# Combining two expert outputs: two input tiles' results in one 32 KB store row, an early table load, last stores from SyncE

## The chip, the cores and the metric

The kernel runs on one core of a Trainium2 chip. The core has several engines, each with its own instruction stream: TensorE (not used here), VectorE (DVE in the profile), ScalarE (ACT), GpSimd (POOL) and SyncE (SP). Data moves between the chip's main memory (HBM) and the on-chip memory SBUF, which has 128 partitions, by 16 transfer engines (DMA). SyncE and ScalarE each have a queue of their own for such transfers; the instructions that issue them are marked SPq and ACTq in the profile.

The metric is the time of one execution in device microseconds, as a median over runs. Before the change it is 241.34 us (three runs, 241.24 to 241.75). The profiled execution, from its first to its last instruction, spans 240.1 us.

## The reference

```python
batch, seq, hidden, n_experts, k = 16, 1024, 512, 8, 2
"expert_outputs": np.random.randn(batch, seq, k, hidden).astype(np.float32)
"combine_weights": np.random.randn(batch, seq, k).astype(np.float32)

def reference(expert_outputs, combine_weights):
    weights = combine_weights[..., np.newaxis]
    return np.sum(expert_outputs * weights, axis=2).astype(np.float32)
```

Each of the 16 x 1024 = 16384 tokens has two vectors of 512 floats. The output is the first times a weight plus the second times another weight. 67.1 MB are read and 33.6 MB written for two multiplications and one addition per output element.

## The kernel before

The 16384 tokens are dealt out to the partitions: partition p holds the tokens p x 128 to p x 128 + 127 (`per` = 128). One token's two vectors are 4 KB next to each other in memory, and one partition's tokens follow each other.

The outer loop (line 45) runs over 16 tiles `g` of `J` = 8 tokens per partition. A tile's input `et` is 128 partitions x 32 KB, 4096 KB in all; it is loaded by one transfer that SyncE issues (line 48). In main memory one partition's part of it is a single run of 32 KB, and the transfer goes as 128 such rows, 8 on each of the 16 transfer engines. A tile's output `ot` is 128 partitions x 16 KB and leaves in one transfer of 128 rows of 16 KB, issued by ScalarE (line 66). The pools (lines 39 and 40) hold four input tiles and four output tiles, 128 + 64 KB of each partition.

For each token of a tile VectorE multiplies the first vector by its weight into `ot` (line 57, TENSOR_SCALAR), and then adds the second vector times its weight (line 58, SCALAR_TENSOR_TENSOR). The weights are in `wt`, 1 KB per partition, which ScalarE's queue loads at the start (line 43). In the last tile the multiplication is ScalarE's (line 55, ACTIVATE with the weight as scale), so that two engines share that tile; and that tile leaves in three stores of 4, 2 and 2 tokens, as soon as each part is done. ScalarE's first activation needs a table, whose load (ACT_TABLE_LOAD) stands right before it in the instruction stream.

A framework puts in the waits. An engine works through its own instructions in the order of the program text, apart from small exchanges among independent ones on VectorE. SyncE issues the first four loads at once; the load of tile g + 4 waits until VectorE has done with tile g. ScalarE issues the store of a tile when VectorE has written all of it; whatever stands behind it on ScalarE waits with it. In each queue the transfers start in the order of issue.

Of the kernel before, what the change touches and what calls it, by code (L numbers as in the profile page):

```python
# [1 line left out]

# [4 lines left out]


@with_exitstack
def kernel(  # L10
    ctx: ExitStack,
    tc: tile.TileContext,
    expert_outputs: bass.AP,
    combine_weights: bass.AP,
    out: bass.AP,
):


    nc = tc.nc
    b, s, k, h = expert_outputs.shape  # L20
    assert k == 2
    n = b * s
    P = nc.NUM_PARTITIONS
    per = n // P
    assert per * P == n
    eo = expert_outputs.rearrange("b s k h -> (b s) (k h)").rearrange("(p t) f -> p t f", p=P)
    cw = combine_weights.rearrange("b s k -> (b s) k").rearrange("(p t) k -> p (t k)", p=P)
    o = out.rearrange("b s h -> (b s) h").rearrange("(p t) f -> p t f", p=P)

    dt = mybir.dt.float32  # L30
    mult = mybir.AluOpType.mult
    add = mybir.AluOpType.add

    J = 8
    copy = mybir.ActivationFunctionType.Copy
    last = per // J - 1

    wpool = ctx.enter_context(tc.tile_pool(name="w", bufs=1))
    ipool = ctx.enter_context(tc.tile_pool(name="in", bufs=4))
    opool = ctx.enter_context(tc.tile_pool(name="out", bufs=4))  # L40

    wt = wpool.tile([P, per * k], dt)
    nc.scalar.dma_start(out=wt, in_=cw)

    for g in range(per // J):
        et = ipool.tile([P, J, k * h], dt)
        ot = opool.tile([P, J, h], dt)
        nc.sync.dma_start(out=et, in_=eo[:, g * J : (g + 1) * J, :])  # L48
        c0 = 0
        for c in (4, 2, 2) if g == last else (J,):  # L50
            for i in range(c0, c0 + c):
                t = g * J + i
                w0, w1 = wt[:, 2 * t : 2 * t + 1], wt[:, 2 * t + 1 : 2 * t + 2]
                if g == last:
                    nc.scalar.activation(out=ot[:, i, :], in_=et[:, i, 0:h], func=copy, scale=w0)  # L55
                else:
                    nc.vector.tensor_scalar_mul(out=ot[:, i, :], in0=et[:, i, 0:h], scalar1=w0)  # L57
                nc.vector.scalar_tensor_tensor(  # L58
                    out=ot[:, i, :],
                    in0=et[:, i, h : 2 * h],  # L60
                    scalar=w1,
                    in1=ot[:, i, :],
                    op0=mult,
                    op1=add,
                )
            nc.scalar.dma_start(  # L66
                out=o[:, g * J + c0 : g * J + c0 + c, :], in_=ot[:, c0 : c0 + c, :]
            )
            c0 += c


# [1 line left out]
_INS = ['expert_outputs', 'combine_weights']  # L73
_OUTS = [((16, 1024, 512), 'float32')]


# [23 lines left out]
```

## Time and profile before

| | |
|---|---|
| time, median of three runs | 241.34 us |
| span of the profiled execution | 240.1 us |
| VectorE busy | 133.8 us (56%) |
| ScalarE busy | 6.4 us (3%) |
| bytes moved | 100.81 MB, 420 GB/s over the span |
| VectorE, line 57 | 120 times, 482 ns each |
| VectorE, line 58 | 128 times, 746 ns each |
| ScalarE, line 55 | 8 times, 709 ns each, and a table load of 1283 ns |
| first compute | at 13.92 us |
| last load's data used from | 227.81 us |

The profile page has six parts: busy times by engine; the span in 40 slices of 6 us each, with the transfer engines' busy share in tenths and the GB/s that they moved; the transfer queues; the chain of work that ended last; the costliest groups of instructions, with the idle time before them and what ended it; and the transfer issues, with the time from issue to landing. An engine that idles much may still not matter: what counts is what the chain at the end waits for. A stretch of the span can be asked for by itself; its row gives busy times, transfer share and GB/s in that stretch. Transfers are counted there at the start of each row, so that a stretch of few microseconds can show a share a little above 1.

### The profile page before, as it was taken

The numbers are of one execution on the slowest core, as the hardware profiler recorded it, in microseconds if no ns is written. First come the engines' busy times: TensorE is split into PE (matmuls) and PEld (weight loads), VectorE is DVE, ScalarE is ACT, GpSimd is POOL, SyncE is SP. The second block draws the span as 40 slices with busy tenths as digits, with TensorE's granted clock in tenths as the row PEclk, the third lists the DMA queues.
The fourth block names the chain that finished last, engine by engine and source line by source line (L and its number), as shares of the span: only waits on it lengthen the run. The fifth ranks groups of instructions, "written<-read, shape, count | busy, mean of one in ns | idle before, by whom it ended". The sixth has DMA issues, their size and how long they took to land.

```text
span 240.1 us, 377 instructions
## 1 busy us (share of the span) xinstructions
DVE 133.8 (56%) x248; ACT 6.4 (3%) x9; POOL 0.2 (0%) x4
## 2 busy tenths in 40 slices
DVE  0068937729185490945819276391853919549062
ACT  0000000000000000000000000000000000000072
POOL 0000000000000000000000000000000000000000
DMA  7999999999999999999999999999999999999967
GB/s 267 439 434 431 355 434 456 414 431 437 437 423 445 439 409 426 456 415 453 420 437 431 415 448 423 431 450 437 435 423 434 420 429 442 418 450 437 412 296 304
DMA packets 5042, 100.81 MB, mean 420 GB/s; under 512 B 560, under 2 KB 688, under 8 KB 944
## 3 DMA queue, kind: packets, MB, share of 16 engines
q1 hardware_dynamic: 2304, 67.11, 65.4%
q10 hardware_dynamic: 2736, 33.69, 32.9%
q14 instruction: 2, 0.02, 0.0%
HBM read 67.24 MB, written 33.55 MB: 420 GB/s over the span
## 4 chain that ended last, share of the span: by engine, by line
DMA 56%; DVE 26%; another core or an unknown queue 13%; issue 1%; ACT 1%; SPq 0%; ACTq 0%; DVEq 0%
DMA et<-in_expert_outputs_dram 56%; DVE ot L58 16%; DVE ot L57 10%; ACT ot L55 1%; ACT L55 1%; SPq L48 0%; ACTq L66 0%; DVEq L95 0%; DVEq L57 0%; ACTq L55 0%
## 5 line engine op out<-in xcount | busy, mean ns | idle before, releaser
L57 DVE TENSOR_SCALAR ot<-et,wt 128x512 f32<-128x512 f32 x120 | 52.7, 482 | 93.4 <-DMA et<-in_expert_outputs_dram 79.5
L58 DVE SCALAR_TENSOR_TENSOR ot<-et,wt,ot 128x512 f32<-128x512 f32 x128 | 90.0, 746 | 9.3 <-ACT ot L55 9.3
L55 ACT ACT_TABLE_LOAD x1 | 1.3, 1283 | 227.8 <-DMA et<-in_expert_outputs_dram 227.8
L55 ACT ACTIVATE ot<-et,wt 128x512 f32<-128x512 f32 x8 | 5.1, 709 | 1.5 <-DVE ot L58 1.5
L84 POOL MEMSET const-bfloat16-1.0<- 128x1 bf16 x1 | 0.1, 101 | 0.0
L84 POOL MEMSET const-uint8-127<- 128x1 uint8 x1 | 0.1, 101 | 0.0
L84 POOL MEMSET const-float32-0.0<- 128x1 f32 x1 | 0.1, 98 | 0.2 <-issue 0.2
L84 POOL MEMSET const-float32-1.0<- 128x1 f32 x1 | 0.1, 98 | 0.0
## 6 DMA issues: line engine op xcount, KB each, us to landing
et<-in_expert_outputs_dram SPq DMA_DIRECT2D x16, 4096.0 KB, 49.6
out_dram<-ot ACTq DMA_DIRECT2D x15, 2048.0 KB, 24.9
out_dram<-ot ACTq DMA_DIRECT2D x1, 1024.0 KB, 3.9
out_dram<-ot ACTq DMA_DIRECT2D x2, 512.0 KB, 3.2
wt<-in_combine_weights_dram ACTq DMA_DIRECT2D x1, 128.0 KB, 13.2
```

The lines of the kernel that those rows point to most:

```text
L55: nc.scalar.activation(out=ot[:, i, :], in_=et[:, i, 0:h], func=copy, scale=w0)
L57: nc.vector.tensor_scalar_mul(out=ot[:, i, :], in0=et[:, i, 0:h], scalar1=w0)
L58: nc.vector.scalar_tensor_tensor(out=ot[:, i, :], in0=et[:, i, h : 2 * h], scalar=w1, in1=ot[:, i, :], op0=mult, op1=add,)
L84: nc = _bacc.Bacc("TRN2", target_bir_lowering=False, num_devices=1)
```

## The change

The change has four parts.

- **Two tiles in one store.** An output tile now holds the results of two input tiles (128 partitions x 32 KB). ScalarE stores it in one transfer of rows of 32 KB when the second of the two tiles is done. There are seven such stores, for tiles 0 to 13. Tile 14 leaves alone, with rows of 16 KB, and tile 15 in four stores of 2 tokens each (rows of 4 KB). The purpose is fewer and longer rows.
- **Three input and three double output tiles** in place of four and four, 96 + 96 KB of each partition, so that the same room suffices.
- **Table loaded early.** The first token of tile 0 is multiplied on ScalarE, so that the table load stands near the start and no longer ahead of the last tile.
- **Last stores from SyncE.** The four stores of tile 15 are issued by SyncE, which has no loads left by then. ScalarE doesn't wait for VectorE between its multiplications of the last tile.

```diff
+    STORES = {t: 2 * J for t in range(2 * J, per, 2 * J)}
+    STORES[per - J] = J
+    STORES.update({t: 2 for t in range(per - J + 2, per + 1, 2)})
...
-    ipool = ctx.enter_context(tc.tile_pool(name="in", bufs=4))
-    opool = ctx.enter_context(tc.tile_pool(name="out", bufs=4))
+    ipool = ctx.enter_context(tc.tile_pool(name="in", bufs=3))
+    opool = ctx.enter_context(tc.tile_pool(name="out", bufs=3))
...
     for g in range(per // J):
         et = ipool.tile([P, J, k * h], dt)
-        ot = opool.tile([P, J, h], dt)
         nc.sync.dma_start(out=et, in_=eo[:, g * J : (g + 1) * J, :])
-        c0 = 0
-        for c in (4, 2, 2) if g == last else (J,):
-            for i in range(c0, c0 + c):
...
-                if g == last:
...
+        if g % 2 == 0:
+            ot = opool.tile([P, 2 * J, h], dt)
+        at = g % 2 * J
+        for i in range(J):
+            t = g * J + i
...
+            if t == 0 or g == last:
+                nc.scalar.activation(out=ot[:, at + i, :], in_=et[:, i, 0:h], func=copy, scale=w0)
+            else:
+                nc.vector.tensor_scalar_mul(out=ot[:, at + i, :], in0=et[:, i, 0:h], scalar1=w0)
...
+            c = STORES.get(t + 1)
+            if c:
+                (nc.sync if g == last else nc.scalar).dma_start(
+                    out=o[:, t + 1 - c : t + 1, :], in_=ot[:, at + i + 1 - c : at + i + 1, :]
                 )
-            nc.scalar.dma_start(
-                out=o[:, g * J + c0 : g * J + c0 + c, :], in_=ot[:, c0 : c0 + c, :]
-            )
-            c0 += c
```

More of the change, by code (lines that the diff above doesn't have):

```diff
@@ L32 @@
     add = mybir.AluOpType.add
+    copy = mybir.ActivationFunctionType.Copy
     J = 8
-    copy = mybir.ActivationFunctionType.Copy
     last = per // J - 1
+    STORES = {t: 2 * J for t in range(2 * J, per, 2 * J)}
+    STORES[per - J] = J
+    STORES.update({t: 2 for t in range(per - J + 2, per + 1, 2)})
     wpool = ctx.enter_context(tc.tile_pool(name="w", bufs=1))
-    ipool = ctx.enter_context(tc.tile_pool(name="in", bufs=4))
-    opool = ctx.enter_context(tc.tile_pool(name="out", bufs=4))
+    ipool = ctx.enter_context(tc.tile_pool(name="in", bufs=3))
+    opool = ctx.enter_context(tc.tile_pool(name="out", bufs=3))
     wt = wpool.tile([P, per * k], dt)
@@ L46 @@
         et = ipool.tile([P, J, k * h], dt)
-        ot = opool.tile([P, J, h], dt)
         nc.sync.dma_start(out=et, in_=eo[:, g * J : (g + 1) * J, :])
-        c0 = 0
-        for c in (4, 2, 2) if g == last else (J,):
-            for i in range(c0, c0 + c):
-                t = g * J + i
-                w0, w1 = wt[:, 2 * t : 2 * t + 1], wt[:, 2 * t + 1 : 2 * t + 2]
-                if g == last:
[L55 to L64, printed above, removed]
-                )
-            nc.scalar.dma_start(
-                out=o[:, g * J + c0 : g * J + c0 + c, :], in_=ot[:, c0 : c0 + c, :]
-            )
-            c0 += c
+        if g % 2 == 0:
[3 more added lines that the diff above has]
+            t = g * J + i
+            w0, w1 = wt[:, 2 * t : 2 * t + 1], wt[:, 2 * t + 1 : 2 * t + 2]
+            if t == 0 or g == last:
+                nc.scalar.activation(out=ot[:, at + i, :], in_=et[:, i, 0:h], func=copy, scale=w0)
+            else:
+                nc.vector.tensor_scalar_mul(out=ot[:, at + i, :], in0=et[:, i, 0:h], scalar1=w0)
+            nc.vector.scalar_tensor_tensor(
+                out=ot[:, at + i, :],
+                in0=et[:, i, h : 2 * h],
+                scalar=w1,
+                in1=ot[:, at + i, :],
+                op0=mult,
+                op1=add,
+            )
+            c = STORES.get(t + 1)
+            if c:
+                (nc.sync if g == last else nc.scalar).dma_start(
+                    out=o[:, t + 1 - c : t + 1, :], in_=ot[:, at + i + 1 - c : at + i + 1, :]
+                )
 _INS = ['expert_outputs', 'combine_weights']
```

## The prediction, before the result was known

> **What bounds the kernel now.** First I read the page's busy times, slices and queues, to see whether an engine or the transfers fill the span. In the queue lines the last column is time in the transfer engines, as a share of 16 engines' span; q1 holds the loads (SyncE), q10 the table and the stores (ScalarE).
>
> ```profile
> DVE 133.8 (56%) x248; ACT 6.4 (3%) x9; POOL 0.2 (0%) x4
> ...
> DMA  7999999999999999999999999999999999999967
> GB/s 267 439 434 431 355 434 456 414 431 437 437 423 445 439 409 426 456 415 453 420 437 431 415 448 423 431 450 437 435 423 434 420 429 442 418 450 437 412 296 304
> ...
> q1 hardware_dynamic: 2304, 67.11, 65.4%
> q10 hardware_dynamic: 2736, 33.69, 32.9%
> ```
>
> VectorE is busy 56%; the transfer engines are busy 65.4 + 32.9 = 98.3%. Only the first slice, the fifth (355) and the last two fall short. So I read those by stretches (columns: stretch, its length, busy us of the engines with their instruction counts, TensorE clock, transfer engines' busy share, GB/s).
>
> ```profile
> 6.00:23.00 17.00, 8.56 (x16) 0.00 (x0) 0.00 (x0) 1.00 1.01 436
> 23.00:28.00 5.00, 4.54 (x9) 0.00 (x0) 0.00 (x0) 1.00 0.94 344
> 28.00:227.80 199.80, 115.27 (x216) 0.00 (x0) 0.00 (x0) 1.00 1.00 432
> 227.80:231.40 3.60, 1.55 (x3) 3.58 (x5) 0.00 (x0) 1.00 1.01 432
> 231.40:233.40 2.00, 2.00 (x4) 1.48 (x3) 0.00 (x0) 1.00 0.14 57
> 233.40:240.10 6.70, 1.94 (x3) 1.33 (x2) 0.00 (x0) 1.00 0.77 313
> ```
>
> From 28 to 227.8 us, when the last load lands, the rate is flat at 432 GB/s with the share at 1.00. Two places stand out: 23 to 28 us, where the engines count as busy but move only 344, and the hole at 231.4 to 233.4. The tail itself is in the order of time (start, duration, engine, line):
>
> ```profile
> 221.78 0.34 ACTq L66 DMA_DIRECT2D out_dram<-ot  x1
> 227.81 1.28 ACT L55 ACT_TABLE_LOAD   x1 [227.81 <-DMA et<-in_expert_outputs_dram]
> 229.10 3.78 ACT L55 ACTIVATE ot<-et,wt 128x512 f32<-128x512 f32 x6
> 229.85 4.07 DVE L58 SCALAR_TENSOR_TENSOR ot<-et,wt,ot 128x512 f32<-128x512 f32 x6 [8.11 <-ACT ot L55]
> 232.63 1.66 ACTq L66 DMA_DIRECT2D out_dram<-ot  x2
> 234.34 1.33 ACT L55 ACTIVATE ot<-et,wt 128x512 f32<-128x512 f32 x2 [1.46 <-DVE ot L58]
> ```
>
> The table load stands on the path, and ScalarE waits in its own store issues before the last two multiplies. Finally the issues with their time to landing:
>
> ```profile
> et<-in_expert_outputs_dram SPq DMA_DIRECT2D x16, 4096.0 KB, 49.6
> out_dram<-ot ACTq DMA_DIRECT2D x15, 2048.0 KB, 24.9
> ```
>
> **Prices.** One transfer engine carries 8 rows of each transfer (128 partitions over 16 engines). A 32 KB load row: 65.4% of 240.1 us is 157.0 us, by 128 rows = 1.227 us. A 16 KB store row: 32.9% is 79.0, less about 5.4 for the table and the small last stores, by 120 = 0.613 us. The packet records of the trace have medians of 1.213, 0.611, 0.313 (8 KB) and 0.160 us (4 KB), which I use. One input tile with one store is 8 x (1.213 + 0.611) = 14.6 us, which is the spacing of the tiles in the chain (37.76, 52.36). A store lands 24.9 us after issue, longer than 14.6: so **the next store is always queued before the last has drained**; ScalarE's queue never runs empty between 23 us and the tail.
>
> **What the Trainium skill says.** DMA: Bandwidth & Descriptors, "Queues, rings and completion order", has each transfer engine taking turns between the queue rows that have work, a packet at a time. The trace agrees: 8 load rows with 8 store rows make the 14.6 us. It follows that the row size sets the shares: 2:1 for the loads now, 1:1 with 32 KB store rows. The same page, "Where 436 GB/s comes from", gives a ceiling of 435 GB/s; measured are 432 to 436, so nothing is left in the steady part. "Issuing engines are not separate DMA queues" there says that another issuing engine saves only issue time (here 0.33 to 0.36 us). ScalarE: Activation LUTs, "What ACT_TABLE_LOAD costs", gives about 1283 ns and a drain of about 1380; the trace has 1283 ns and no gap after it (229.10 follows 227.81 + 1.28). No page says what it costs a busy transfer engine when a queue goes from empty to filled.
>
> **The change, part by part.**
>
> *Double stores.* Per transfer engine 112 rows of 16 KB become 56 of 32 KB. Two 16 KB rows cost 2 x 0.611 = 1.222, one of 32 KB 1.213: 56 x 0.009 = **0.5 us less**, on the path, since the engines are the bound. In the last tile 4 stores of 4 KB rows (32 x 0.160 = 5.12) replace 8 x 0.313 + 16 x 0.160 = 5.06: 0.06 us more.
>
> *The double stores' rhythm.* A pair of tiles is 16 load rows and 8 store rows, 24 x 1.213 = 29.1 us. A store, one for one with loads, is through in 16 x 1.213 = 19.4 us, and then the queue is **empty for 9.7 us** until the next. So it fills from empty seven times, where before it did once (22.51 us). What that once cost is visible: 23 to 28 us moved 344 instead of 432 GB/s, 5 x (1 - 344/432) = 1.0 us lost. Packet records: at that place the load rows on all 16 engines stretch from 1.21 to as much as 2.0 us, 0.72 us of extra time per engine, and this ahead of the first store row, so before store data moves. The instruction queue's two 8 KB fetches (47.4 and 173.7 us) each likewise stretch the load row behind them, by 0.54 and 0.60 us. Against it: the store queue starts only once beside loads in this trace, so it may be a first-time cost. Bounds: 0 to 1.0 us a restart; I take 0.72. Six more restarts: **+4.3 us** (0 to 6).
>
> *Three input tiles.* A load now waits for VectorE three tiles back. VectorE takes 8.5 us a tile (13.92 to 22.45), and loads alone bring a tile in 8 x 1.213 = 9.7 us. While tile g is computed, g+1 and g+2 are queued, 19.4 us of work for loads alone: the load queue doesn't empty. Cost nothing, hidden by the queued loads. The third double output tile back has landed tens of us before VectorE writes it again. Semaphores shared among transfers add waits on SyncE for older stores; by the order of the instructions each is for one issued at least 30 us earlier. Nothing.
>
> *Table early.* 1.28 us leaves 227.81 and lies beside the first tile, where VectorE starts with rows 1 and 2 and needs ScalarE's row later. *Last stores from SyncE.* ScalarE's 8 multiplies then run through (0.63 us apart) and VectorE ends about 8 x 0.67 + 0.75 = 6.1 us after the last load; before it was 236.5 - 227.8 = 8.7. That takes 2.6 us off the compute path. But how much of it counts? At the last load's landing some 4.2 MB remain (store of tile 14 and all of tile 15), 9.7 us at 432: the transfers, not ScalarE, end last. What is saved is their hole. And the hole (0.14 busy for 2 us) is not one on all engines: the records show one engine, the one delayed by the instruction fetches, busy through to 233.36, and idle then for only 0.1 us and 0.25 us at 237.3. The slowest engine sets the end, so **0.35 us saved**, where the window suggests 1.7. The first SyncE store also starts an empty queue, beside tile 14's: 0 to 0.7, taken as 0.2.
>
> Sum: -0.5 + 0.06 - 0.35 + 4.3 + 0.2 = +3.7; 241.34 + 3.7 = **245.0 us**.
>
> **Rivals.**
> A, restarts cost (the forecast): 245.0. For it: the stall at 23 to 28 us, on all engines, at the one place where a queue fills beside a busy one, and the fetches' like stalls.
> B, the 23 us stall belongs to the very first store: no restart costs. Then -0.5 + 0.06 - 0.35 = -0.8: **240.5 us**, faster. For it: the tail's first small store shows no stretched row (but there no other queue was at work).
> C, a restart costs about 0.3 us, as part of the stall was start-up: -0.8 + 6 x 0.3 + 0.1 = +1.1, **242.4 us**.
> D, the whole hole counts, all engines finishing together: -0.5 + 0.06 - 1.7 = -2.1, **239.2 us**. Against it: the one late engine.
>
> **How the numbers follow.** A 0.50, B 0.33, C 0.10, D 0.07. Within 0.2% (0.48 us) of no change lie B with a small restart cost on top, 0.04, and a low C, 0.01. So same 0.05, faster 0.33 + 0.07 - 0.04 = 0.36, slower 0.50 + 0.10 - 0.01 = 0.59. The range has to hold B as well as A: 240.2 (B less 0.3) to 246.3 (A with about 0.93 us a restart).
>
> **What would show it.** Restarts: dips in GB/s with the share at 1.00, one per double store, about 29 us apart, from about 32 us on; the steady stretch below 432 by some 2%. Rhythm: stores of 4096 KB landing in some 20 us, tiles' starts spaced 10 and 19 us by turns instead of 14.6. Tail: no table load after the last landing, ScalarE's 8 multiplies in one run, transfer share near 1.00 up to the end. Table load near 14 us, with tile 0 no later than before. If the steady stretch holds 432 GB/s, A is wrong and B or D is left, told apart by how full the tail is. Loads waiting on VectorE or on a store, with a share under 1.00 in mid-span, would break the argument on three input tiles.

## The result, and the profile after

The changed kernel takes 244.91 us (median of six runs, 243.43 to 246.27); the kernel before, run beside it, 241.55. The ratio is 1.0139, 95% interval 1.01 to 1.0179: slower by 3.4 us. The runs of the changed kernel lie 2.8 us apart, those of before 0.6; the latter fall into two groups, near 241.2 and near 241.8 us, and the profiled run of before (241.88 us) is of the upper one.

The page of the changed kernel, with the parts that answer to those shown of before:

```profile
DVE 133.3 (55%) x247; ACT 7.0 (3%) x10; POOL 0.2 (0%) x4
...
DMA  7999999999999999999999999999999999999993
GB/s 264 445 407 437 437 361 431 427 437 431 405 437 431 421 431 421 437 431 431 437 431 431 431 431 431 410 433 437 431 437 431 426 426 431 431 388 431 423 394 143
DMA packets 4178, 100.81 MB, mean 415 GB/s; under 512 B 464, under 2 KB 592, under 8 KB 1104
...
q1 hardware_dynamic: 2880, 69.21, 67.5%
q10 hardware_dynamic: 1296, 31.59, 30.2%
```

The same bytes go in fewer packets (4178 for 5042), one multiplication has moved from VectorE to ScalarE, and the transfer engines are full through the middle as before. But there are dips in the GB/s, at slices 3, 6, 11, 26 and 36 (407, 361, 405, 410, 388), and the last slice falls to 143. I then read stretches of 4 us where a double store comes in (the first seven rows), two stretches between them, and the end; the last line covers all that follows the first dip, up to the last load's landing. The columns are those of the stretches of before.

```profile
33.00:37.00 4.00, 3.38 (x7) 0.00 (x0) 0.00 (x0) 1.00 1.03 360
60.50:64.50 4.00, 0.86 (x3) 0.00 (x0) 0.00 (x0) 1.00 0.99 385
92.00:96.00 4.00, 2.89 (x7) 0.00 (x0) 0.00 (x0) 1.00 0.97 385
120.00:124.00 4.00, 1.52 (x4) 0.00 (x0) 0.00 (x0) 1.00 1.01 426
151.00:155.00 4.00, 3.02 (x7) 0.00 (x0) 0.00 (x0) 1.00 0.99 393
179.00:183.00 4.00, 1.12 (x3) 0.00 (x0) 0.00 (x0) 1.00 0.95 410
212.00:216.00 4.00, 3.55 (x7) 0.00 (x0) 0.00 (x0) 1.00 0.99 385
...
124.00:151.00 27.00, 15.59 (x30) 0.00 (x0) 0.00 (x0) 1.00 1.00 432
...
183.00:212.00 29.00, 15.99 (x30) 0.00 (x0) 0.00 (x0) 1.00 1.01 432
...
229.70:238.00 8.30, 5.39 (x8) 5.01 (x8) 0.00 (x0) 1.00 0.96 402
238.00:243.00 5.00, 0.00 (x0) 0.00 (x0) 0.00 (x0) 1.00 0.21 86
...
38.00:229.70 191.70, 106.86 (x200) 0.00 (x0) 0.00 (x0) 1.00 1.00 428
```

Two things are to be seen. Where a double store comes in, the engines count as busy but move less than 432: 360 at the first, 385 to 393 at four others, nearly nothing lost at 120 to 124. Over the whole stretch behind the first dip the rate is 428, where before it was 432, which is 1.8 us in 191.7. And after 238 us the transfer share is 0.21: most transfer engines have ended and a few still work, for 3.7 us. The order of time shows the tail's compute (start, duration, engine, line):

```profile
13.79 1.28 ACT L63 ACT_TABLE_LOAD   x1 [13.79 <-DMA et<-in_expert_outputs_dram]
...
229.76 5.01 ACT L63 ACTIVATE ot<-et,wt 128x512 f32<-128x512 f32 x8 [213.96 <-DMA et<-in_expert_outputs_dram]
230.51 5.39 DVE L66 SCALAR_TENSOR_TENSOR ot<-et,wt,ot 128x512 f32<-128x512 f32 x8 [9.51 <-ACT ot L63]
231.96 4.32 SPq L77 DMA_DIRECT2D out_dram<-ot  x4
```

The table load has left the tail, ScalarE's eight multiplies run through in 5.01 us, VectorE is done at 235.9 and the last store issued at 236.3. All this is as the change meant it; yet the last row ends at 241.7.

**The account by packet records.** A record of the trace is one row on one transfer engine. I sum over all, by 16, and take off rows x median duration; what is over the median is called stretched. The records do not name their engine, but each engine's part of a transfer ends with a record of 4 bytes, which tells when that part landed. Numbers are us per transfer engine, for the profiled runs (spans of 240.1 and 243.0 us).

| | before | after | difference |
|---|---|---|---|
| rows at their median durations | 234.02 | 233.57 | -0.45 |
| rows stretched, first store | 0.74 | 0.79 | +0.05 |
| rows stretched, the six later double stores | - | 1.8 | +1.8 |
| rows stretched at 12 to 18 us | 0 | 0.32 | +0.32 |
| idle, 6 us to 225 us | 0.0 | 0.12 | +0.12 |
| idle, 225 us to the last row's end | 1.86 | 2.65 | +0.79 |

The sum is +2.6, of the +2.85 by which the last row ends later (238.83 and 241.68); the rest I put down to small stretches. As far as the records can be put in line by their times, most of the stretched time (2.1 of the 2.4 us in load rows after 20 us) lies in load rows that stand one or two rows ahead of a double store's first row on the same engine. The idle time at the end has changed its kind. Before, it was the hole at 231.4 to 233.4, in which 15 engines waited for the first part of the last tile. After, it is unequal ends: the parts of load 15 (the last; the first is load 0) land over 9.0 us among the 16 engines (220.4 to 229.4), where before they landed within 2.6 (224.7 to 227.3), and in the last store two engines end 2.9 and 2.6 us later than the middle one. The spread of the landings grows in the course of the run (2.1 us at load 3, 5.2 at load 11), where before it stayed at 1.8 from load 2 to load 11. On their last rows the engines are only 3.5 us apart (238.1 to 241.7), so the 9.0 us are in part another order of load and store rows.

### The profile page after: what moved, and what is told of

The parts are those of the page before. It is cut to its first block, busy times and chain, and to the rows that moved or that the text cites. A ratio compares the mean times of both kernels' runs of the same rounds, so it can differ in the third digit from the quotient of the medians.

```text
span 243.0 us, 360 instructions
## 1 busy us (share of the span) xinstructions
DVE 133.3 (55%) x247; ACT 7.0 (3%) x10; POOL 0.2 (0%) x4
## 2 busy tenths in 40 slices
DMA packets 4178, 100.81 MB, mean 415 GB/s; under 512 B 464, under 2 KB 592, under 8 KB 1104
## 4 chain that ended last, share of the span: by engine, by line
DMA 77%; DVE 19%; ACT 0%; DVEq 0%; issue 0%; SPq 0%
DMA et<-in_expert_outputs_dram 71%; DVE ot L66 13%; DVE ot L65 7%; DMA wt<-in_combine_weights_dram 5%; ACT ot L63 0%; DVEq L105 0%; SPq L53 0%
## 5 line engine op out<-in xcount | busy, mean ns | idle before, releaser
L63 ACT ACTIVATE ot<-et,wt 128x512 f32<-128x512 f32 x9 | 5.7, 709 | 214.0 <-DMA et<-in_expert_outputs_dram 214.0
```

The lines of the kernel that those rows point to most:

```text
L63: nc.scalar.activation(out=ot[:, at + i, :], in_=et[:, i, 0:h], func=copy, scale=w0)
```

## The experiments

Each ran beside the kernel before. Ratios are to it, with their 95% intervals.

**1. Which part of the change costs?** Four kernels, each with one part done or undone.

Double stores and three double tiles alone, the tail as before:

```diff
-    STORES.update({t: 2 for t in range(per - J + 2, per + 1, 2)})
+    STORES.update({per - 4: 4, per - 2: 2, per: 2})
...
-            if t == 0 or g == last:
+            if g == last:
...
-                (nc.sync if g == last else nc.scalar).dma_start(
+                nc.scalar.dma_start(
```

> The changed kernel without its tail parts: first token on VectorE, table load late, last tile in stores of 4, 2 and 2 tokens from ScalarE. Double stores and three double tiles alone. If the double stores are the whole loss: 244.5 - 245.5 us. If the SyncE stores in the tail (a queue that restarts beside tile 14's store) carry part: 242.5 - 244.

Measured: 244.05 us, ratio 1.0121 (1.0091 to 1.015), between the two ranges expected. The interval overlaps that of the whole change, so the double stores are the loss, or most of it. Its stretches show the same dips:

```profile
33.00:37.00 4.00, 3.79 (x8) 0.00 (x0) 0.00 (x0) 1.00 1.03 328
...
92.00:96.00 4.00, 3.12 (x7) 0.00 (x0) 0.00 (x0) 1.00 0.93 393
...
211.00:215.00 4.00, 3.43 (x7) 0.00 (x0) 0.00 (x0) 1.00 1.00 369
124.00:151.00 27.00, 15.04 (x29) 0.00 (x0) 0.00 (x0) 1.00 1.01 433
```

The tail parts alone, on the kernel before:

```diff
-        for c in (4, 2, 2) if g == last else (J,):
+        for c in (2, 2, 2, 2) if g == last else (J,):
...
-                if g == last:
+                if t == 0 or g == last:
...
-            nc.scalar.dma_start(
+            (nc.sync if g == last else nc.scalar).dma_start(
```

> The kernel before with the two tail parts alone: first token on ScalarE (table load near 14 us), last tile in four stores from SyncE. My step: -0.3 us (the slowest transfer engine sets the end), 241.0 - 241.5. Rival D: the whole hole is saved, -1.7, 239.8. Rival G: the table load near 14 us stalls loads (half of the engines have a stretched load row there in the changed kernel, 0.3 us on average) and unequal ends cost: 242 and up.

Measured: 241.47 us, ratio 0.9999 (0.9991 to 1.0008). The hole is filled, as its stretch in the place of the hole shows, and nothing measurable is gained:

```profile
231.50:233.50 2.00, 2.00 (x4) 1.28 (x3) 0.00 (x0) 1.00 0.97 397
233.50:238.00 4.50, 0.42 (x1) 0.00 (x0) 0.00 (x0) 1.00 0.74 301
```

By the records 15 engines now end at 236.3 to 237.3 us, and one at 238.3. That one had almost no hole to lose.

Three input and three output tiles, on the kernel before (`bufs=4` to `bufs=3` in both pools):

> The kernel before with three input and three output tiles. My step: no cost, 241.3 - 241.9 us. Rival: fewer loads in flight cost 1 us or more (242.5 and up).

Measured: 241.72 us, ratio 1.0002 (0.9993 to 1.0011). The buffers cost nothing.

The double stores undone, all else of the change kept. The store becomes two stores of one tile each:

```diff
-                (nc.sync if g == last else nc.scalar).dma_start(
-                    out=o[:, t + 1 - c : t + 1, :], in_=ot[:, at + i + 1 - c : at + i + 1, :]
-                )
+                for c0 in range(0, c, J):
+                    n = min(c, J)
+                    (nc.sync if g == last else nc.scalar).dma_start(
+                        out=o[:, t + 1 - c + c0 : t + 1 - c + c0 + n, :],
+                        in_=ot[:, at + i + 1 - c + c0 : at + i + 1 - c + c0 + n, :],
+                    )
```

> The changed kernel, with each double store issued as two stores of one tile, rows of 16 KB, at the same moment as before. Rhythm, buffers and tail stay; the store queue then needs 16 x (1.213 + 0.611) = 29.2 us for what comes every 29.2 us, so it doesn't run empty. Theory A (a queue that fills from empty beside a busy one stalls the transfer engines): the stalls from the second store on go, and the time falls from 244.9 to 240.5 - 242 us. Rival E (the loss is in the tail, in the engines' unequal ends after the change there, or in the three input tiles): stays at 244 - 245.5. Rival F (32 KB rows are slow in themselves): falls too, but the load rows would show no stretching in the changed kernel; they do.

Measured: 241.43 us, ratio 0.9996 (0.9988 to 1.0005). The loss is gone, and the rate in the middle is back at 432:

```profile
28.00:227.20 199.20, 115.69 (x217) 0.00 (x0) 0.00 (x0) 1.00 1.00 432
```

But the expectation described the kernel wrongly: each tile's store waits only for its own tile, so the first left at 22.05 us and not with its pair at 32.5. It undoes pairs and row size together. A second try was to keep the moments, with the second tile's half first in the text (`for c0 in (J, 0) if c > J else (0,)`):

> The changed kernel, with each double store issued as two stores with rows of 16 KB, the second tile's half first, so that both leave only when the second tile is done. Same moments as in the changed kernel, but the store queue now needs 29.2 us of every 29.2 and doesn't empty. If empty spells of the queue bring the stalls (A): like before, 241 - 242 us. If it is the bunching of stores in pairs, whatever their rows: 244 - 245.5.

Measured: 241.46 us, ratio 0.9999 (0.9991 to 1.0007). The framework put the first tile's store first again (issued at 22.16 us), so this is the same kernel in effect, and 16 KB rows leaving in pairs beside 32 KB load rows were not tried.

**2. Is it enough that the store queue runs empty?** This is theory A as it was forecast. Two kernels with rows of 16 KB make it run empty.

Loads in two halves of 16 KB rows, on the kernel before:

```diff
-        nc.sync.dma_start(out=et, in_=eo[:, g * J : (g + 1) * J, :])
+        for half in range(2):
+            a, z = half * J // 2, (half + 1) * J // 2
+            nc.sync.dma_start(out=et[:, a:z, :], in_=eo[:, g * J + a : g * J + z, :])
```

> The kernel before, with each load issued as two loads of 4 tokens, rows of 16 KB, so that stores and loads take turns one for one at equal size. A store is through in 16 x 0.611 = 9.8 us of every 14.7, and the store queue fills from empty 16 times in place of once. More rows cost 128 x 0.009 = 1.1 us. Theory A: +1.1 and 15 restarts of 0.3 to 0.7 us, +5.5 to +11: 247 - 252 us, with dips in GB/s at each store. If the stall belongs to the first store or to 32 KB store rows: 242 - 243 us.

Measured: 242.78 us, ratio 1.0058 (1.0043 to 1.0074), close to what the rows alone cost (1.1 us). By the records the store queue filled from empty ten times, not 16, since two tiles' stores mostly followed each other closely; before most of the later fills it had been dry for some 8 us, before two of them for 2.4. The stretches at the first and at three later refills:

```profile
20.00:24.00 4.00, 2.85 (x6) 0.00 (x0) 0.00 (x0) 1.00 0.94 287
49.50:53.50 4.00, 3.54 (x7) 0.00 (x0) 0.00 (x0) 1.00 1.01 414
...
108.50:112.50 4.00, 3.57 (x7) 0.00 (x0) 0.00 (x0) 1.00 1.01 434
137.50:141.50 4.00, 3.78 (x7) 0.00 (x0) 0.00 (x0) 1.00 1.03 438
```

The first refill is dear, 287 GB/s (1.2 us per engine by the records); the second costs 0.2 and the rest nothing.

Half of the stores left out, on the kernel before:

```diff
+            if g % 2 == 0 or g == last:
...
```

> The kernel before, without the stores of the odd tiles 1 to 13 (so half of the output isn't written). The store queue empties for some 9.7 us ahead of each of 8 stores, with rows of 32 KB in loads and 16 KB in stores. By rows: 241.3 less 56 x 0.611 = 34.2, so 207.1 us if restarts cost nothing beyond the first. If restarts beside 32 KB load rows stall by 0.3 to 0.7 us: 209 - 212 us.

Measured: 207.97 us (207.82 to 208.85), 0.9 over the sum by rows. At the first store and at three later refills:

```profile
24.00:28.00 4.00, 4.00 (x9) 0.00 (x0) 0.00 (x0) 1.00 0.89 332
47.00:51.00 4.00, 2.23 (x5) 0.00 (x0) 0.00 (x0) 1.00 0.97 416
...
121.00:125.00 4.00, 3.57 (x7) 0.00 (x0) 0.00 (x0) 1.00 0.97 418
...
170.50:174.50 4.00, 3.64 (x8) 0.00 (x0) 0.00 (x0) 1.00 1.01 434
```

The records have stretched rows at the first store (0.65 us) and none at the later seven. So A in its general form falls: **a store queue of 16 KB rows that runs empty and fills beside loads costs 0.65 to 1.2 us the first time in these two kernels, and at most 0.2 us later.** The stall at 23 to 28 us before (0.74 us) was of that first kind.

**3. Is it the row size, then?** Four kernels with store rows of 32 KB and more.

32 KB store rows beside 16 KB load rows: the edit of the loads above, on the changed kernel.

> The changed kernel with each load issued as two loads with rows of 16 KB; stores stay at 32 KB rows and their queue stays empty half of the time. Rows alone: +1.1 us. If 32 KB load rows are needed for the stalls: 241.5 - 242.5 us. If the 32 KB store rows bring them: 245 - 246.5 us.

Measured: 244.59 us, ratio 1.0122 (1.0102 to 1.0141), so 32 KB load rows are not needed for the loss. Taking off some 1.1 us for rows, it is smaller than the changed kernel's. The stretched rows come late (from 175 us on), not at each double store, and more than half of that time is in store rows; the landings of one load again spread over 6 us. Set beside the loads in 16 KB rows of experiment 2, this kernel says something on row size: there the stores, in 16 KB rows, mostly left in runs of two tiles too, with the queue dry for some 8 us between runs, and that took 242.78 us. The 1.8 us between the two come with the store row. They also differ in buffers and tail, which cost nothing by themselves above, and 0.8 of the 1.8 us is more idle time after 225 us.

48 KB store rows, three tiles to a store, five stores:

```diff
-    STORES = {t: 2 * J for t in range(2 * J, per, 2 * J)}
-    STORES[per - J] = J
+    STORES = {t: 3 * J for t in range(3 * J, per, 3 * J)}
...
-    opool = ctx.enter_context(tc.tile_pool(name="out", bufs=3))
+    opool = ctx.enter_context(tc.tile_pool(name="out", bufs=2))
...
-        if g % 2 == 0:
-            ot = opool.tile([P, 2 * J, h], dt)
-        at = g % 2 * J
+        if g % 3 == 0:
+            ot = opool.tile([P, 3 * J, h], dt)
+        at = g % 3 * J
```

> The changed kernel with three input tiles' outputs in one store of 48 KB rows: five stores (tiles 0 to 14) in place of seven and one, two triple output tiles; input, table and tail unchanged. Rows alone: about -0.2 us against the changed kernel. If each store that meets an empty queue costs some 0.3 to 0.5 us whatever its size: four restarts beyond the first in place of six, 243.5 - 244.5 us. If the loss grows with the store row's size: 245.5 us and up. If 32 KB rows were a special case: 241 - 242.

Measured: 243.56 us, ratio 1.0083 (1.0068 to 1.0098): fewer restarts, smaller loss, and no growth with the row. By the records each of the later refills but the last has load rows stretched by 0.4 to 0.5 us per engine, and the 48 KB rows themselves are stretched by 0.65 us in all. Its end differs: the last load has landed by 220.6 us, the last 48 KB store is issued only at 219.92 and its rows start at 220.8, and the engines idle for some 1.5 us each just before. From there to the last row they work without a gap. So the time alone doesn't give the cost of a restart.

Each double store followed at once by a second one, so that the queue never runs dry between them:

```diff
+                if c == 2 * J:
+                    u = ((t + 1) // c + 4) % 7 * c
+                    nc.scalar.dma_start(out=o[:, u : u + c, :], in_=ot)
```

> The changed kernel, with each of the seven double stores followed at once by a second 4096 KB store of the same tile into another pair's place in the output (so the output isn't the reference's). Rows of 32 KB stay, 56 more per transfer engine, but the store queue then has 16 rows for every 16 load rows and doesn't empty. By rows: 244.9 + 56 x 1.213 = 312.8 us if all losses stay; 3.4 us less, 309.4, if they come from 32 KB store rows that meet an empty queue (A, narrowed to 32 KB rows). At or above 312.8: 32 KB store rows cost without an empty queue too. In the trace: stretched rows at the first store alone, or at every store.

Measured: 310.89 us (309.48 to 312.53). The median is halfway between 309.4 and 312.8, but the six runs cover almost all of that distance. After the first store the rate over all the middle is 430 GB/s:

```profile
33.00:37.00 4.00, 3.79 (x8) 0.00 (x0) 0.00 (x0) 1.00 1.04 377
37.00:290.00 253.00, 110.62 (x206) 3.93 (x7) 0.00 (x0) 1.00 1.00 430
```

By the records the store queue doesn't run empty here, and the rows stretched after the first store add up to some 1.3 us per engine, spread over many places, in place of 1.8 at six. So rows of 32 KB lose something without a dry queue, and A, even narrowed to long rows, is only a part of the story. How large a part, these six runs and one trace don't settle.

One queue for loads and double stores, on the changed kernel:

```diff
-                (nc.sync if g == last else nc.scalar).dma_start(
+                (nc.scalar if c == J else nc.sync).dma_start(
```

> The changed kernel with the double stores issued by SyncE, in line with the loads (tile 14's store stays on ScalarE). 32 KB rows and pairs stay; there is one queue, so no store meets a running queue and each transfer engine does the same rows in the same order. If the loss comes from two queues meeting with 32 KB rows: 240.5 - 242 us, with load landings within 2 us of each other among the engines. If from 32 KB store rows in themselves: 244 - 246. A queue that runs dry would show as transfer share under 1.00.

Measured: 255.68 us, ratio 1.0595 (1.0576 to 1.0613). It settles nothing on the loss, since SyncE now held loads back behind a store that waits for VectorE, and the queue ran dry:

```profile
62.00:70.00 8.00, 6.84 (x14) 0.00 (x0) 0.00 (x0) 1.00 0.79 336
```

One thing stands out all the same: rows stretch by 0.9 to 1.2 us per engine in each of the first six rounds, with no second queue at work, where the double store's rows end and load rows follow (41 to 46 us in the first round).

**4. The late transfer engine.** The account of the tail said that one transfer engine, held up by two instruction fetches, sets the end. It does so twice over: a load has landed only when its last engine is done, and of load 15 the middle engine was done at 225.3 us, the late one at 227.3, just before the tail's compute began. So I took work out of VectorE's instruction stream: every first multiplication on ScalarE, the tail as in the change, stores of one tile.

```diff
...
-                if g == last:
+                if True:
                     nc.scalar.activation(out=ot[:, i, :], in_=et[:, i, 0:h], func=copy, scale=w0)
...
```

> The kernel before with all first multiplications on ScalarE (line 55's instruction for every token) and the last tile in four stores from SyncE. VectorE then has 128 instructions in place of 248. My account of before says that the end is set by the one transfer engine that the two instruction fetches delay by 1.7 us in all. If the fetches go: 240.2 - 240.9 us. If the fetches stay or another engine is as late: 241.2 - 241.7.

Measured: 240.57 us (nine runs, 240.49 to 241.01), ratio 0.9967 (0.9957 to 0.9978): the one kernel here that does all of the work and beats the kernel before, by 0.8 us at the mean of the runs. It beats the one with the tail parts alone by 0.9 and the changed one by 4.3. Its groups:

```profile
L58 DVE SCALAR_TENSOR_TENSOR ot<-et,wt,ot 128x512 f32<-128x512 f32 x128 | 86.3, 747 | 147.3 <-ACT ot L55 147.3
L55 ACT ACTIVATE ot<-et,wt 128x512 f32<-128x512 f32 x128 | 80.1, 708 | 137.3 <-DMA et<-in_expert_outputs_dram 137.3
```

The time is in the range expected for a kernel without fetches, yet they have not gone; there are two still, at 93.4 and 100.7 us. But in load 15 the last of the 16 engines is only 0.9 us after the middle one (2.0 before, 1.6 with the tail parts alone), and the last rows end within 236.3 and 237.4. The landings by engine show why: the two fetches fall on different engines now. Behind the first, one engine goes from 0.1 to 0.7 us after the middle one; behind the second, another goes from 0.1 to 0.9. Before, one and the same engine went from 1.1 to 2.0 at its second fetch. That the gain is due to this alone is not shown, since the work of VectorE and ScalarE changed with it.

## Why the prediction came out as it did

The forecast was 245.0 us, slower, by case A; measured 244.91. As a difference, +3.7 was forecast and +3.4 measured. Direction, size and the origin in the double stores were right. The rhythm came as forecast too: by the records the two queues' rows mostly took turns one by one, a double store was worked off in 17 to 20 us, and then no store row followed for 7 to 13 us. The closeness of the sum, though, is luck: two of its terms were wrong in opposite directions.

- **Six restarts at 0.72 us, +4.3.** The stretched rows are there, at the places forecast (the first store's from 34 to 39 us, then about every 29 us), but uneven: 0.38, 0.31, 0.07, 0.36, 0.19 (nearly all of it in store rows) and 0.49 us, in sum 1.8 in place of 4.3. The steady stretch fell by 0.9%, from 432 to 428, where some 2% were expected. The step that failed is reading the 23 us stall as the price of every restart. It was mainly the price of the first store: with 16 KB store rows and the loads unchanged, seven later refills had no stretched row. Rival B had that right for the old row size, and wrong for the new one. Of the price of a restart, C (0.3 us) was nearest.
- **The tail, -0.35 and +0.2.** That the hole was worth little was right: the tail parts alone gave 0.9999, and D's 1.7 us are refuted, since the late engine had almost no hole. But the forecast took the engines' unequal progress for fixed. With 32 KB store rows beside 32 KB load rows, the landings of one load spread to 9 us, and idle time at the end grows by 0.79 us where the sum had it shrink by 0.15. It grows as much (by 0.8) in the kernel with the double stores alone. This was in no rival.
- **Packets, -0.5 + 0.06.** Measured -0.45, as forecast.
- **Three input tiles, nothing.** Right (1.0002).
- **Table early, nothing.** Right for compute: tile 0 is not later. Half of the engines have a stretched row at 12 to 18 us (0.32 us on average); the kernel with the stores undone has it too (0.28), the one with the tail parts alone has not, and neither has the second try at pairs, which is in effect the kernel with the stores undone. So it comes and goes from run to run; I did not find its cause.

What stays open: why rows stretch where store rows of 32 KB come in and why the engines' landings spread, while with 16 KB rows they don't after the first time, even when the queue runs dry. Shown is that the double stores bring the loss, that buffers and tail don't, and that a dry queue alone doesn't. That a filled queue removes a part of the loss is likely, but its size isn't known. Pairs of stores with 16 KB rows at the changed kernel's moments beside 32 KB load rows, which would part row size from bunching cleanly, were not run; the two kernels with 16 KB load rows speak for row size.

## What to carry to other kernels

When 98% of the span is transfer, longer rows are worth only their few nanoseconds per row (0.009 us here, 0.5 us in all), and what they bring with them can cost more: here 3.4 us in all. 16 KB store rows against 32 KB load rows, in the 1:2 ratio of the bytes, kept both queues filled and the engines within 2.6 us of each other. A stall seen once is not the price of each repetition; look for a kernel in which it repeats before multiplying it. And a hole in the mean transfer share is worth only what the last of the 16 engines has of it: here 0.35 of 1.7 us at most, of which nothing could be measured.

## What the runs showed that I had not expected

The first store of a kernel beside running loads costs 0.5 to 1.2 us per transfer engine (0.74 before, 0.79 after, 1.2 with 16 KB load rows), later ones with 16 KB rows 0 to 0.2. An 8 KB instruction fetch held up one transfer engine by some 0.9 us in the kernel before (0.31 for its row, 0.53 to 0.60 for the load row behind it) and by 0.55 to 0.84 in the last kernel above, and two of them on one engine had a large part in the end of the kernel before. Kernels with 32 KB store rows beside 32 KB load rows vary from run to run: six runs of each spread over 2.8 us for the whole change, 2.7 for the double stores alone and 3.1 where the store queue stays filled, against 0.6 before. So the spread doesn't need a queue that restarts; with 48 KB rows it was 0.5.
